# A 4 KB store of zeros ahead of the first rows of a softmax-minus-one-hot kernel

## The chip, the cores and the metric

The kernel runs on one core of one Trainium2 chip. The metric is the device time of one execution in microseconds (us): the median of 3 runs is 1248.03 us (1248.02 to 1248.24). The profile comes from one further execution.

The engines are named as in the profile: PE is TensorE, DVE is VectorE, ACT is ScalarE, POOL is GpSimd, SP is SyncE. SyncE computes nothing here; it issues DMAs. A DMA is issued on the queue of an engine (q1 is SyncE's, q10 ScalarE's in the profile), and the work of both queues runs on the same 16 DMA engines.

## The reference

Logits are 8 x 1024 rows of 8192 float32 numbers, labels one integer for each row.

```python
logits_max = np.max(logits, axis=-1, keepdims=True)
exp_logits = np.exp(logits - logits_max)
softmax = exp_logits / np.sum(exp_logits, axis=-1, keepdims=True)
one_hot[batch_idx, seq_idx, labels] = 1.0
return (softmax - one_hot).astype(np.float32)
```

So 268 MB are read and 268 MB written, and every number is touched by a maximum, an exponential with a sum, a scaling, and a subtraction of 1 where the column is the label.

## The kernel before

**Tiles.** The 8192 rows are cut into T = 64 tiles of 128 rows ("row t" in the code and below: one tile of 128 x 8192 float32, 4.194 MB). Two neighbouring tiles form a block b = t // 2, with j = t % 2. SBUF holds X, three slots of two tiles; block b lives in slot b % 3, so six tiles are on the chip at a time, and tile t uses the memory of tile t - 6.

**Instructions.** All instructions are recorded through the helper `run` (lines 63 to 74): it puts the instruction on an engine in program order, lets it wait on the semaphores in its list, and counts a semaphore up when it ends. So the order within each engine is the order of the calls, and between engines only the listed waits hold. In the profile nearly everything has line L68, that of the helper, and is told apart by engine, operation and tile.

**Before the loop** (lines 77 to 101). ScalarE issues the load of the labels (64 KB as 32 rows of 2 KB). GpSimd sets `ident`, a 32 x 32 tile, to zero (memset), makes it the identity (affine_select), and writes column numbers 0 to 8191 as 16-bit integers (iota) into the memory of X that tile 5 is going to use (`made`). VectorE turns the labels to float (`lab_f`), TensorE transposes them with `ident`, VectorE copies the result out of PSUM (`lab`) and copies `made` into PSUM (`iota`); this last copy needs GpSimd's iota. VectorE's own order is: cast, copy of `lab`, copy of `iota`, and then the maximum of row 0.

**Loads.** SyncE issues the loads of tiles 0 to 5 at once, tile 5 after the copy of `iota`, since `made` lies in its memory. Every later load t waits for the store of tile t - 6. All loads are in order on SyncE's queue, which carries nothing else.

**The loop over the tiles.** For each t, VectorE does the reciprocal of row t's sum, the maximum of row t + 1 (tensor_reduce to `m`), and the subtraction for row t (scalar_tensor_tensor: is the column number equal to the label, minus the scaled row, reversed). ScalarE does the exponential of row t with its sum, issues the store of row t - 1, and scales row t by the reciprocal. The last row is scaled, subtracted and stored in pieces: four column quarters, two stores of half a row. At the end ScalarE waits for the last six tiles' stores.

Of the kernel before, what the change touches and what calls it, by code (L numbers as in the profile page):

```python
# [7 lines left out]
P = 128  # L8
G = 2
SLOTS = 3  # L10


LOADS = "r" * 32
LAST = 4


# [1 line left out]
def kernel(  # L18
# [6 lines left out]
    nc = tc.nc  # L25
# [3 lines left out]
    Act = mybir.ActivationFunctionType  # L29
    Alu = mybir.AluOpType  # L30

    x_nv = logits.flatten_outer_dims()
    o_nv = out.flatten_outer_dims()
    N, V = x_nv.shape
    T = N // P
    B = T // G
    lab_bp = labels.rearrange("a b -> (a b)").rearrange("(b q) -> b q", q=G * P)
    x_b = x_nv.rearrange("(b p j) v -> b p j v", p=P, j=G)
    o_b = o_nv.rearrange("(b p j) v -> b p j v", p=P, j=G)
# [5 lines left out]
    X = const.tile([P, SLOTS, G, V], fp32)  # L45
    lab_raw = const.tile([B, G * P], labels.dtype)
    lab_f = const.tile([B, G, P], fp32)
    ident = const.tile([B, B], fp32)
    lab = const.tile([P, G, B], fp32)

    m, s, r = (const.tile([P, T], fp32, name=n) for n in ("m", "s", "r"))

    iota = psum.tile([P, V], i16)
    lab_ps = iota[:].bitcast(fp32)[:, :T].rearrange("p (j b) -> p j b", j=G)

    with tc.tile_critical():  # L56
        sem = tc.alloc_semaphore
        got = [[sem(f"got{i}{q}") for q in range(2)] for i in range(SLOTS)]
        put = [[sem(f"put{i}{q}") for q in range(2)] for i in range(SLOTS)]
        lab_got, dve, act, pe, pool = (sem(n) for n in ("lab_got", "dve", "act", "pe", "pool"))  # L60
        count = {}

        def run(engine, waits, counter, method, **operands):

            waits = list(dict.fromkeys(waits))
            for w in waits[:-1]:
                engine.wait_ge(*w)
            instruction = getattr(engine, method)(**operands)  # L68
            for w in waits[-1:]:
                instruction._wait_ge(*w)  # L70
            step = 16 if method == "dma_start" else 1
            instruction.then_inc(counter, step)
            count[counter.name] = count.get(counter.name, 0) + step
            return counter, count[counter.name]


        w_raw = run(nc.scalar, [], lab_got, "dma_start", out=lab_raw[:], in_=lab_bp)
        w = run(nc.gpsimd, [], pool, "memset", ap=ident[:], constant=0.0)
        w_ident = run(
            nc.gpsimd, [w], pool, "affine_select",  # L80
            out=ident[:], in_=ident[:], compare_op=Alu.not_equal, fill=1.0,
            base=0, pattern=[[-1, B]], channel_multiplier=1,
        )

        made = X[:, SLOTS - 1, G - 1, :].bitcast(i16)[:, :V]
        w_made = run(
            nc.gpsimd, [], pool, "iota", out=made, pattern=[[1, V]], base=0, channel_multiplier=0
        )
        step = mybir.dt.size(labels.dtype) // 4
        lab32 = lab_raw[:].bitcast(i32).rearrange("b (p j s) -> b j p s", j=G, s=step)  # L90
        w_lab = run(nc.vector, [w_raw], dve, "tensor_copy", out=lab_f[:], in_=lab32[:, :, :, 0])
        for j in range(G):
            w = run(
                nc.tensor, [w_ident, w_lab], pe, "transpose",
                out=lab_ps[:, j, :], in_=lab_f[:, j, :], identity=ident[:],
            )
        w_turned = run(nc.vector, [w], dve, "tensor_copy", out=lab[:], in_=lab_ps)
        w_iota = run(
            nc.vector, [w_turned, w_made], dve, "tensor_scalar",
            out=iota[:].bitcast(i32), in0=made.bitcast(i32), scalar1=0, scalar2=None, op0=Alu.bitwise_or,  # L100
        )


        every, rows = slice(0, P), slice(0, G)
        one = [slice(j, j + 1) for j in range(G)]
        halves = [slice(i, P, 2) for i in range(2)]
        PIECES = {
            "r": [(every, js) for js in one],
            "s": [(ps, js) for js in one for ps in halves],
            "t": [(ps, one[0]) for ps in halves] + [(every, js) for js in one[1:]],  # L110
            "w": [(every, rows)],
        }

        def meets(a, b):

            sets = [[set(range(*d.indices(n))) for d, n in zip(p, (P, G))] for p in (a, b)]
            return all(x & y for x, y in zip(*sets))


        loaded, stored, finished = {}, {}, []  # L120
        last_made = [((every, slice(G - 1, G)), w_iota)]

        def load(b):
            loaded[b] = []
            before = stored.get(b - SLOTS, last_made if b == SLOTS - 1 else [])
            for piece in PIECES[LOADS[b]]:
                ps, js = piece
                free = [w for other, w in before if meets(piece, other)]
                queue = nc.scalar if ps == halves[1] else nc.sync
                w = run(  # L130
                    queue, free, got[b % SLOTS][js.start], "dma_start",
                    out=X[ps, b % SLOTS, js, :], in_=x_b[b, ps, js, :],
                )
                loaded[b].append((piece, w))

        def store(t, done, c=slice(0, V)):
            b, j = divmod(t, G)
            piece = (every, one[j])
            w = run(
                nc.scalar, [done], put[b % SLOTS][j], "dma_start",  # L140
                out=o_b[b, :, j, c], in_=X[:, b % SLOTS, j, c],
            )
            stored.setdefault(b, []).append((piece, w))


        def row(t):
            return X[:, t // G % SLOTS, t % G, :]

        def row_max(t):
            b, j = divmod(t, G)  # L150
            arrived = {w[0].name: w for piece, w in loaded[b] if meets(piece, (every, one[j]))}
            return run(
                nc.vector, arrived.values(), dve, "tensor_reduce",
                out=m[:, t : t + 1], in_=row(t), axis=mybir.AxisListType.X, op=Alu.max, negate=True,
            )


        for b in range(SLOTS):
            load(b)
        w_max = row_max(0)  # L160
        for t in range(T):
            x = row(t)
            label = lab[:, t % G, t // G : t // G + 1]
            w = run(
                nc.scalar, [w_max], act, "activation",
                out=x, in_=x, func=Act.Exp, bias=m[:, t : t + 1], scale=1.0, accum_out=s[:, t : t + 1],
            )
            w_sum = run(nc.vector, [w], dve, "reciprocal", out=r[:, t : t + 1], in_=s[:, t : t + 1])
            if t + 1 < T:
                if (t + 1) % G == 0 and (t + 1) // G >= SLOTS:  # L170
                    load((t + 1) // G)
                w_max = row_max(t + 1)
            if t > 0:
                store(t - 1, finished[t - 1])

            n = 1 if t + 1 < T else LAST
            cols = [slice(i * V // n, (i + 1) * V // n) for i in range(n)]
            scaled = [
                run(
                    nc.scalar, [w_sum], act, "activation",  # L180
                    out=x[:, c], in_=x[:, c], func=Act.Copy, bias=0.0, scale=r[:, t : t + 1],
                )
                for c in cols
            ]
            done = [
                run(
                    nc.vector, [w], dve, "scalar_tensor_tensor",
                    out=x[:, c], in0=iota[:, c], scalar=label, in1=x[:, c],
                    op0=Alu.is_equal, op1=Alu.subtract, reverse1=True,
                )  # L190
                for c, w in zip(cols, scaled)
            ]
            finished.append(done[-1])
        half = V // 2
        store(T - 1, done[LAST // 2 - 1], slice(0, half))
        store(T - 1, done[LAST - 1], slice(half, V))
        for b in range(B - SLOTS, B):
            last = {w[0].name: w for _, w in stored[b]}
            for w in last.values():
                nc.scalar.wait_ge(*w)  # L200


# [28 lines left out]
```

## Time and profile before

| what | value |
|---|---|
| median of 3 runs | 1248.03 us |
| the profiled execution | 1248.17 us, of it 1246.4 us span |
| DVE / ACT / POOL busy | 1121.6 / 919.4 / 7.4 us |
| bytes moved by DMA, mean rate | 536.98 MB, 431 GB/s |
| loads on SP's queue | 64, 4096 KB each, median 24.2 us from issue to landing |
| stores on ACT's queue | 63, 4096 KB each, median 55.1 us; two of 2048 KB |
| the labels' load on ACT's queue | 64 KB, 3.9 us |

The span runs from the first to the last instruction of the program; the execution's own time has some 1.8 us around it. "40 slices" are 40 equal parts of the span, 31 us each, in which a digit is the busy share in tenths. In the groups, the numbers behind the bar are the busy time in us and the mean of one instruction in ns, then the idle time of the engine just before such instructions and what ended it. In a row of the windows there stand the stretch in us, its length, the busy time of PE, PEld, DVE, ACT and POOL with the number of instructions, the granted clock, the DMA share and, last, GB/s. A window counts a DMA packet where it starts, so short windows scatter. The trace also keeps every DMA packet by itself, with its start, duration, bytes and queue; a tile moves as 128 packets of 32 KB, eight on each of the 16 DMA engines, and each transfer ends with one packet of 4 bytes for each engine, which counts the semaphore up.

### The profile page before, as it was taken

The page shows a single profiled execution, that of the slowest core. Times are in us where ns is not written, and L with a number is a line of the kernel's source. Part 1 is how long each engine was busy: PE and PEld are TensorE (multiplying, and loading weights), DVE is VectorE, ACT ScalarE, POOL GpSimd, SP SyncE. Part 2 cuts the span into 40 slices and gives each one's busy share as a digit, 9 for nine tenths or more (in the row PEclk, how much of TensorE's full clock was granted, in tenths as well). Part 3 has the DMA queues.
Part 4 walks back from the last instruction along what each step waited for, and adds up shares of the span by engine and source line. Part 5 has one row for each costly group of instructions (what it writes and reads, how often), then busy time and mean ns, then how long its engine had stood idle before and what let it go on. Part 6 is the DMA issues. An engine that isn't in the chain of part 4 may idle for free.

```text
span 1246.4 us, 597 instructions
## 1 busy us (share of the span) xinstructions
PE 0.4 (0%) x2; PEld 0.3 (0%) x2; DVE 1121.6 (90%) x198; ACT 919.4 (74%) x196; POOL 7.4 (1%) x7
## 2 busy tenths in 40 slices
PE   0000000000000000000000000000000000000000
PEld 0000000000000000000000000000000000000000
DVE  5999999999988989889898898998988989889893
ACT  3888888888767777677767777777777777677772
POOL 2000000000000000000000000000000000000000
DMA  9999999999999999999999999999999999999998
GB/s 406 415 430 433 436 433 430 434 435 433 432 433 434 433 432 433 434 432 433 433 434 432 433 433 433 433 433 433 434 433 431 434 434 433 430 433 436 432 430 387
DMA packets 18628, 536.98 MB, mean 431 GB/s; under 512 B 2080, under 2 KB 2080, under 8 KB 2112
## 3 DMA queue, kind: packets, MB, share of 16 engines
q1 hardware_dynamic: 9216, 268.44, 50.0%
q10 hardware_dynamic: 9408, 268.51, 49.9%
q14 instruction: 4, 0.03, 0.0%
HBM read 268.50 MB, written 268.44 MB: 431 GB/s over the span
## 4 chain that ended last, share of the span: by engine, by line
another core or an unknown queue 69%; DVE 21%; DMA 6%; SPq 1%; ACT 1%; DVEq 0%; issue 0%; PE 0%; ACTq 0%
DVE m L68 10%; DVE X L68 10%; DMA out_dram<-X 4%; DMA X<-in_logits_dram 2%; SPq L68 1%; ACT X L68 1%; DVE iota L68 0%; DMA lab_raw<-in_labels_dram 0%; DVE lab_f L68 0%; DVEq L56 0%; DVE r L68 0%; PE iota L68 0%; ACTq L68 0%; DVE lab L68 0%
## 5 line engine op out<-in xcount | busy, mean ns | idle before, releaser
L68 DVE TENSOR_REDUCE m<-X 128x1 f32<-128x8192 f32 x64 | 555.5, 8680 | 91.4 <-DMA X<-in_logits_dram 91.4
L68 ACT ACTIVATE X<-X,m 128x8192 f32<-128x8192 f32 x64 | 455.8, 7122 | 187.9 <-DVE m L68 187.9
L68 DVE SCALAR_TENSOR_TENSOR X<-iota,lab,X 128x8192 f32<-128x8192 int16 (+1 forms) x67 | 559.8, 8359 | 2.4 <-ACT X L68 2.4
L68 ACT ACTIVATE X<-X,r 128x8192 f32<-128x8192 f32 (+1 forms) x67 | 456.3, 6815 | 116.0 <-DVE r L68 116.0
L68 DVE RECIPROCAL r<-s 128x1 f32<-128x1 f32 x64 | 9.7, 152 | 7.3 <-ACT X L68 7.3
L68 ACT ACTIVATION_READ_ACCUMULATOR X<-X,m 128x1 f32 x64 | 11.9, 187 | 0.0
L68 DVE CAST lab_f<-lab_raw 32x256 f32<-32x256 int32 x1 | 3.6, 3610 | 4.8 <-DMA lab_raw<-in_labels_dram 4.8
L68 POOL IOTA X<- 128x8192 int16 x1 | 6.9, 6944 | 0.0
L68 DVE TENSOR_SCALAR iota<-X 128x4096 int32<-128x4096 int32 x1 | 4.4, 4428 | 0.1
L68 ACT ACT_TABLE_LOAD x1 | 1.3, 1283 | 1.4 <-SPq L56 1.4
L68 DVE COPY lab<-iota 128x64 f32<-128x64 f32 x1 | 0.2, 225 | 0.5 <-PE iota L68 0.5
L68 PE MATMUL iota<-ident,lab_f 32*128 32x32 f32 x2 | 0.4, 299 | 8.5 <-DVE lab_f L68 8.5
L68 PEld LDWEIGHTS iota<-ident,lab_f 32*128 32x128 f32 x2 | 0.3, 196 | 8.5 <-DVE lab_f L68 8.5
L68 POOL TENSOR_SCALAR_AFFINE_SELECT ident<-ident 32x32 f32<-32x32 f32 x1 | 0.2, 203 | 0.1
L68 POOL MEMSET ident<- 32x32 f32 x1 | 0.1, 115 | 0.5 <-SPq L56 0.5
L215 POOL MEMSET const-bfloat16-1.0<- 128x1 bf16 x1 | 0.1, 107 | 0.0
L215 POOL MEMSET const-uint8-127<- 128x1 uint8 x1 | 0.1, 107 | 0.0
L215 POOL MEMSET const-float32-0.0<- 128x1 f32 x1 | 0.1, 104 | 0.2 <-issue 0.2
L215 POOL MEMSET const-float32-1.0<- 128x1 f32 x1 | 0.1, 104 | 0.0
## 6 DMA issues: line engine op xcount, KB each, us to landing
X<-in_logits_dram SPq DMA_DIRECT2D x64, 4096.0 KB, 24.2
out_dram<-X ACTq DMA_DIRECT2D x63, 4096.0 KB, 55.1
out_dram<-X ACTq DMA_DIRECT2D x2, 2048.0 KB, 16.8
lab_raw<-in_labels_dram ACTq DMA_DIRECT2D x1, 64.0 KB, 3.9
```

Of the source, the lines that this page charges most:

```text
L68: instruction = getattr(engine, method)(**operands)
L215: nc = _bacc.Bacc("TRN2", target_bir_lowering=False, num_devices=1)
```

## The change

A third transfer is added to the start. After the labels, ScalarE's queue gets a store of `ident` while it is still all zeros: 32 rows of 128 bytes into the first 32 columns of the first 32 rows of the output. It waits for GpSimd's memset. GpSimd's affine_select, which turns the zeros into the identity, then waits until this store has landed, with a semaphore of its own, `early`. The store of row 0, which writes the same places of the output again with the right numbers, waits for `early` too.

The rest of the diff writes the loop in other functions: loads are issued tile by tile (`load(t)`) in place of block by block, unused ways to cut a load (`PIECES`, `LOADS`) go, and the last row's scalings and subtractions are called in turn.

```diff
+        w_early = run(
+            nc.scalar, [w], early, "dma_start", out=o_nv[0:B, 0:B], in_=ident[:]
+        )
         w_ident = run(
-            nc.gpsimd, [w], pool, "affine_select",
+            nc.gpsimd, [w, w_early], pool, "affine_select",
             out=ident[:], in_=ident[:], compare_op=Alu.not_equal, fill=1.0,
             base=0, pattern=[[-1, B]], channel_multiplier=1,
         )
...
+        def load(t):
+            b, j = divmod(t, G)
+            free = [stored[t - G * SLOTS]] if b >= SLOTS else [w_iota] if t == G * SLOTS - 1 else []
+            loaded[t] = run(
+                nc.sync, free, got[b % SLOTS][j], "dma_start", out=row(t), in_=x_b[b, :, j, :]
+            )
...
         def store(t, done, c=slice(0, V)):
             b, j = divmod(t, G)
...
+            stored[t] = run(
+                nc.scalar, [w_early, done] if t == 0 else [done], put[b % SLOTS][j], "dma_start",
+                out=o_b[b, :, j, c], in_=row(t)[:, c],
+            )
...
+        def by_rows(first, last):
+            for t in range(first, last):
+                row_exp(t)
+                invert(t, t + 1)
+                if t + 1 < T:
+                    if t + 1 >= G * SLOTS:
+                        load(t + 1)
+                    row_max(t + 1)
+                if t > 0:
+                    store(t - 1, finished[t - 1])
+                if t + 1 < T:
+                    row_scale(t)
+                    subtract(t)
...
+        for t in range(G * SLOTS):
+            load(t)
+        row_max(0)
+        by_rows(0, T)
+        quarters = [slice(i * V // 4, (i + 1) * V // 4) for i in range(4)]
+        done = []
+        for c in quarters:
+            row_scale(T - 1, c)
+            done.append(subtract(T - 1, c))
```

Here B is 32, G is 2, SLOTS is 3 and T is 64. `row_exp`, `invert`, `row_max`, `row_scale` and `subtract` each record one instruction, the one that stood in the loop before.

More of the change, by code (lines that the diff above doesn't have):

```diff
@@ L10 @@
 SLOTS = 3
-LOADS = "r" * 32
 LAST = 4
@@ L59 @@
         put = [[sem(f"put{i}{q}") for q in range(2)] for i in range(SLOTS)]
-        lab_got, dve, act, pe, pool = (sem(n) for n in ("lab_got", "dve", "act", "pe", "pool"))
+        lab_got, dve, act, pe, pool, early = (
+            sem(n) for n in ("lab_got", "dve", "act", "pe", "pool", "early")
+        )
         count = {}
@@ L101 @@
         )
[L104 to L117, printed above, removed]
@@ L120 @@
[L120 to L134, printed above, removed]
+        stored, loaded, finished, biggest, summed, inverse, scaled = {}, {}, {}, {}, {}, {}, {}
@@ L136, in store, with row @@
+        def row(t):
+            return X[:, t // G % SLOTS, t % G, :]
+        def load(t):
[4 more added lines that the diff above has]
+            )
         def store(t, done, c=slice(0, V)):
             b, j = divmod(t, G)
[L138 to L141, printed above, removed]
-            )
@@ L143, in store @@
-            stored.setdefault(b, []).append((piece, w))
-        def row(t):
-            return X[:, t // G % SLOTS, t % G, :]
+            stored[t] = run(
+                nc.scalar, [w_early, done] if t == 0 else [done], put[b % SLOTS][j], "dma_start",
+                out=o_b[b, :, j, c], in_=row(t)[:, c],
+            )
         def row_max(t):
[L150 to L153, printed above, removed]
+            biggest[t] = run(
+                nc.vector, [loaded[t]], dve, "tensor_reduce",
@@ L154, in row_max @@
                 out=m[:, t : t + 1], in_=row(t), axis=mybir.AxisListType.X, op=Alu.max, negate=True,
             )
[L158 to L166, printed above, removed]
-            )
[L168 to L193, printed above, removed]
@@ L194, with row_exp @@
-        half = V // 2
[L195 to L200, printed above, removed]
+        def row_exp(t):
+            summed[t] = run(
+                nc.scalar, [biggest[t]], act, "activation", out=row(t), in_=row(t),
+                func=Act.Exp, bias=m[:, t : t + 1], scale=1.0, accum_out=s[:, t : t + 1],
+            )
@@ new lines, in invert, with row_scale, subtract @@
+        def invert(a, z):
+            w = run(nc.vector, [summed[z - 1]], dve, "reciprocal", out=r[:, a:z], in_=s[:, a:z])
+            inverse.update((t, w) for t in range(a, z))
+        def row_scale(t, c=slice(0, V)):
+            scaled[t] = run(
+                nc.scalar, [inverse[t]], act, "activation", out=row(t)[:, c], in_=row(t)[:, c],
+                func=Act.Copy, bias=0.0, scale=r[:, t : t + 1],
+            )
+        def subtract(t, c=slice(0, V)):
+            finished[t] = run(
+                nc.vector, [scaled[t]], dve, "scalar_tensor_tensor",
+                out=row(t)[:, c], in0=iota[:, c], scalar=lab[:, t % G, t // G : t // G + 1],
+                in1=row(t)[:, c], op0=Alu.is_equal, op1=Alu.subtract, reverse1=True,
+            )
+            return finished[t]
@@ new lines @@
+        row_max(0)
[5 more added lines that the diff above has]
+            done.append(subtract(T - 1, c))
+        half = V // 2
+        store(T - 1, done[1], slice(0, half))
+        store(T - 1, done[3], slice(half, V))
+        last = {stored[t][0].name: stored[t] for t in range(T - G * SLOTS, T)}
+        for w in last.values():
+            nc.scalar.wait_ge(*w)
```

## The prediction

> **What bounds the kernel now.** I read the page's 40 slices first, then the costliest groups, the waits (of the DMA queues too), the timeline of the first 90 us and the throughput by window.
>
> The 40 slices and three groups of the page:
>
> ```profile
> DVE  5999999999988989889898898998988989889893
> ...
> DMA  9999999999999999999999999999999999999998
> GB/s 406 415 430 433 436 433 430 434 435 433 432 433 434 433 432 433 434 432 433 433 434 432 433 433 433 433 433 433 434 433 431 434 434 433 430 433 436 432 430 387
> ...
> L68 DVE TENSOR_REDUCE m<-X 128x1 f32<-128x8192 f32 x64 | 555.5, 8680 | 91.4 <-DMA X<-in_logits_dram 91.4
> L68 ACT ACTIVATE X<-X,m 128x8192 f32<-128x8192 f32 x64 | 455.8, 7122 | 187.9 <-DVE m L68 187.9
> L68 DVE SCALAR_TENSOR_TENSOR X<-iota,lab,X 128x8192 f32<-128x8192 int16 (+1 forms) x67 | 559.8, 8359 | 2.4 <-ACT X L68 2.4
> ```
>
> The DMA engines are full from the first slice to the last, at 433 GB/s. A tile of 128x8192 f32 is 4.194 MB, so it takes 4.194/433 = 9.68 us, and a row of work (one load, one store) 19.36 us. VectorE needs 8.68 + 8.74 = 17.4 us a row, which is less. The longest wait of SyncE's queue says the same:
>
> ```profile
> SPq L68 <- DMA out_dram<-X: 1141.3, 58, 57.4
> ```
>
> Each of the last 58 loads waits for the store that frees its slot. The kernel therefore ends when 537 MB have gone through. A delay on an engine counts only where it leaves *both* queues (loads on SyncE's, stores on ScalarE's) without data, or makes the DMA engines move less.
>
> The start, where the change sits, from the timeline (start, duration):
>
> ```profile
> 0.91 0.42 ACTq L68 DMA_DIRECT2D lab_raw<-in_labels_dram  x1
> 0.95 0.12 POOL L68 MEMSET ident<- 32x32 f32 x1 [0.51 <-SPq L56]
> ...
> 1.15 0.20 POOL L68 TENSOR_SCALAR_AFFINE_SELECT ident<-ident 32x32 f32<-32x32 f32 x1
> 1.31 6.94 POOL L68 IOTA X<- 128x8192 int16 x1
> ...
> 4.79 3.61 DVE L68 CAST lab_f<-lab_raw 32x256 f32<-32x256 int32 x1 [4.79 <-DMA lab_raw<-in_labels_dram]
> ...
> 9.25 4.43 DVE L68 TENSOR_SCALAR iota<-X 128x4096 int32<-128x4096 int32 x1
> 13.58 8.68 DVE L68 TENSOR_REDUCE m<-X 128x1 f32<-128x8192 f32 x1
> ...
> 64.29 0.34 ACTq L68 DMA_DIRECT2D out_dram<-X  x1
> ```
>
> The last line is the issue of row 1's store; row 0's goes out at 46.98. And the throughput by window (last column GB/s):
>
> ```profile
> 4.00:44.00 40.00, 0.42 (x2) 0.29 (x2) 31.31 (x7) 20.02 (x4) 4.25 (x1) 1.00 1.00 433
> 44.00:56.00 12.00, 0.00 (x0) 0.00 (x0) 12.00 (x4) 9.03 (x4) 0.00 (x0) 1.00 1.01 393
> ...
> 200.00:1198.00 998.00, 0.00 (x0) 0.00 (x0) 907.73 (x158) 747.25 (x159) 0.00 (x0) 1.00 1.00 433
> ```
>
> There is one dip between the ramp and the tail: 44 to 56 us, where the first store begins. It costs 12 x (1 - 393/433) = 1.1 us. The trace's records of single packets show it on all 16 DMA engines: two load packets of 32 KB in a row take 1.5 to 2.1 us instead of 1.21, and the first packet of the store starts at 52.1, 5.15 us after its issue. When the load queue runs dry later (load 6, issued at 71.48, has its first packet at 75.1), the store packets go on at 1.21 us and nothing is lost. So a queue that starts again costs nothing by itself; only the first store did.
>
> **The change part by part.** Per engine, the loop's instructions, operands and order stay the same on SyncE, ScalarE and VectorE: the loads were already issued row by row on a queue that does nothing else, so moving their place in the program moves no wait. The new code is therefore worth 0, apart from these four edits.
>
> 1. *One DMA on ScalarE's queue.* It waits for the memset (done at 1.07), long before the labels' issue ends (1.33). Its own issue takes 0.34 to 0.42 us; behind it stands the table load (1.28 us) of an engine that is idle until 22.3. Cost 0.
>
> 2. *4 KB in 32 pieces of 128 bytes*, two on each DMA engine. The labels' 2 KB pieces took 0.08 us each when undisturbed, so between 0 (4 KB at 433 GB/s is 0.01 us) and 0.2 us of DMA time. I take 0.1.
>
> 3. *affine_select waits until it has landed, and iota stands behind it on GpSimd.* Call the landing L. Lower bound: as fast as the labels (3.85 us from issue to landing): L = 1.33 + 3.85 = 5.2. Upper bound: as late to begin as row 0's store, 5.15 us, then two load packets of 1.21 between its pieces and its semaphore, and 0.7 to land: L = 9.6, or 10.8 if it meets the 1.2 us stall besides. Between them, by the packets: the labels' semaphore ran at 4.1, one load packet after their data, since the two queues take turns by packet. Piece, piece and semaphore behind that, each one load packet of 1.21 later, are at 5.3, 6.5 and 7.7, and 0.5 to land gives L = 8.2, my value. The iota is then ready at L + 0.1 + 0.20 + 6.94 = 15.4. Today the copy of it starts at 9.25, so the first reduce and all rows behind move by d = L - 1.9 = **6.3 us** (3.3 to 8.9). The transposes need ident at about 8.5 and are hidden behind the iota.
>
> What does d cost? Load 5 waits for that copy, but its turn at the DMA engines comes only at 52: cover 38 us. VectorE is late until its lead over the loads is used up (back to back until about 250 us, then 91.4 us of waiting): hidden. The one narrow place is the end of row 0's store. Seven transfers (loads 0 to 5, store 0) end at 72.3 by the packets. The next data are row 1's store, issued at 64.29 + d, with at least 1.06 us to its first packet (as the labels), and load 6, which waits for store 0 to land. So both queues are dry from d = 72.3 - 64.29 - 1.06 = **6.9 us** on. At d = 6.3: 0 us. At 8.9: 2.0 us, then load 6 fills in.
>
> 4. *Row 0's store has one more wait,* met long before: 0.
>
> The Trainium skill ("DMA: Bandwidth & Descriptors", Anatomy of one DMA) puts the fixed cost of a small DMA at about 2.0 us, most of it the receipt of the write, heaviest for HBM. By that figure alone L would be about 3.3 and d an estimated 1.4; the labels' 3.85 us from issue to landing beside full load packets already speak against it, and by either the time stays.
>
> **Sum.** 0 + 0.1 + 0 + 0, and the 1.1 us of the first store is paid once, early or late: +0.1. If the pieces of 128 bytes are a little slower than that, +0.3. The profiled execution took 1248.17 (span 1246.4 and 1.8 around it), 0.14 above the median of 1248.03; I put the sum on the median: **1248.2 us**.
>
> **The rivals.**
>
> *The first store's 1.1 us goes away* because the small store takes it while the DMA engines are ramping up anyway (first load packets of 1.4 to 1.7 us instead of 1.21). For: it came once, at the first write to the output. Against: engines that stall at 3 us stall loads too. Seven transfers then end at 71.2; row 1's store is ready at 64.29 + 6.3 + 1.06 = 71.7: 0.5 us of the gain is lost again. Time 1247.0 to 1247.6; I say 1247.3.
>
> *Paid twice*: the stall belongs to the first write and, again, to the first full packet of a store. Cost 1.1 to 1.2: 1249.3.
>
> *Slower: the rows start so late that both queues run dry.* Mechanism as in 3, place: the end of row 0's store at 72 us. It decides from d = 6.9, and passes 2.5 us from about d = 11.5, L = 13.4: row 1's store is ready 2.5 us or more after the data end, load 6 only at about 74.3 (2.0 us dry), and in the next round store 2 (issued at 81.6 + 12) comes 1.0 us after 93.7, which makes 3.0 us at d = 12: 1251. Each further us adds to it, up to some 5 us at d = 15. For: no row shows a write of 128 bytes, and row 0's store began 5.15 us late. The Trainium skill (same page, Specifications) says that pieces under 512 bytes are written by reading, modifying and writing; no run here shows it yet, and it would push L up. Against: it needs 12 us for 4 KB.
>
> *It does more than hide the stall*: ramp (0.8 us by the packets), stall (1.1) and the spread between the engines at the end (last landings 1243.3 to 1245.1, 1.3 us lost) all gone would be 3.2 us: 1244.8. Nothing speaks for the last.
>
> **How the numbers follow.** Forecast 0.46 (1248.2, between 1247.8 and 1248.8), stall gone 0.21, paid twice 0.17, dry queues 0.12, more than the stall 0.04. A difference under 0.2%, 2.5 us, is about what a measurement of this kernel can tell from none: the first three lie inside, 0.84. Slower 0.12, faster 0.04. The range takes in the first three and the bounds of d: from 1246.8 (the whole 1.1 us gone) to 1250.6 (0.1, 2.0 us dry and a part of the stall twice).
>
> **What the profile after would show.** (3) The small store's landing near 8.2, affine_select behind it, iota at 8.5 to 15.5, first reduce at about 19.9, row 0's store issued at 53.3. (2) 433 GB/s wherever both queues hold data. A dip to about 393 in the 12 us around row 0's store if the stall stays, at 3 to 8 us if it moved. Rivals: no dip anywhere; dips in both places; a dip at 71 to 75 us. I would be wrong if the loads' pace between 200 and 1198 us left 433, which no part of the change touches, or if the small store landed past 13.

## The result

The changed kernel takes 1251.51 us (median of 8 runs, 1250.97 to 1252.38) against 1248.16 for the kernel before (8 runs, 1247.97 to 1248.25): 3.35 us more, a ratio of 1.0028 with a 95% interval of 1.0019 to 1.0036. The forecast was 1248.2 with a range up to 1250.6; the time lies above it. The profiled execution of the changed kernel took 1250.97 us with a span of 1249.2, so 2.80 us more than that of before: it is the fastest of the eight, and what follows accounts for the 2.8 us of that execution, not for all of the 3.35.

From the page of the changed kernel: the throughput in 40 slices, two groups with the idle time before them, and the issue of the small store.

```profile
GB/s 405 420 390 430 435 435 433 431 431 434 434 435 430 431 434 435 435 429 431 434 436 433 430 431 434 436 433 432 433 430 436 434 433 431 432 435 433 433 432 385
...
L69 DVE TENSOR_SCALAR iota<-X 128x4096 int32<-128x4096 int32 x1 | 4.4, 4427 | 6.1 <-POOL X L69 6.1
...
L69 POOL TENSOR_SCALAR_AFFINE_SELECT ident<-ident 32x32 f32<-32x32 f32 x1 | 0.2, 202 | 8.6 <-DMA out_dram<-ident 8.6
...
out_dram<-ident ACTq DMA_DIRECT2D x1, 4.0 KB, 8.2
```

From the fourth slice on it is the old picture, about 433 GB/s up to the last slice (385, before 387). The third slice (62 to 94 us) has 390 in place of 430. The other lines tell how the change gets there: the small store needs 8.2 us from issue to landing, GpSimd's affine_select stands idle for 8.6 us until then, and VectorE waits 6.1 us for the iota behind it.

The timeline of the same execution (start, duration):

```profile
9.66 0.20 POOL L69 TENSOR_SCALAR_AFFINE_SELECT ident<-ident 32x32 f32<-32x32 f32 x1 [8.60 <-DMA out_dram<-ident]
9.82 6.94 POOL L69 IOTA X<- 128x8192 int16 x1
...
16.80 4.43 DVE L69 TENSOR_SCALAR iota<-X 128x4096 int32<-128x4096 int32 x1 [6.14 <-POOL X L69]
21.14 8.68 DVE L69 TENSOR_REDUCE m<-X 128x1 f32<-128x8192 f32 x1
...
54.53 0.36 ACTq L69 DMA_DIRECT2D out_dram<-X  x1
...
71.84 0.35 ACTq L69 DMA_DIRECT2D out_dram<-X  x1
...
72.38 0.33 SPq L69 DMA_DIRECT2D X<-in_logits_dram  x1
```

The first reduce starts at 21.14 in place of 13.58, the stores of rows 0 and 1 go out at 54.53 and 71.84 in place of 46.98 and 64.29: all rows are 7.55 us late. The last line is the issue of load 6, which waits for row 0's store to land.

Throughput by window, first of the kernel before, then of the changed one (last column GB/s):

```profile
68.00:80.00 12.00, 0.00 (x0) 0.00 (x0) 12.00 (x2) 10.85 (x3) 0.00 (x0) 1.00 1.01 434
```

```profile
56.00:68.00 12.00, 0.00 (x0) 0.00 (x0) 12.00 (x2) 10.87 (x2) 0.00 (x0) 1.00 0.99 401
68.00:80.00 12.00, 0.00 (x0) 0.00 (x0) 12.00 (x3) 9.52 (x3) 0.00 (x0) 1.00 0.95 363
80.00:90.00 10.00, 0.00 (x0) 0.00 (x0) 10.00 (x4) 7.67 (x3) 0.00 (x0) 1.00 0.98 423
90.00:130.00 40.00, 0.00 (x0) 0.00 (x0) 40.00 (x7) 34.05 (x7) 0.00 (x0) 1.00 1.00 428
```

The dip of the first store has gone along with it to 56 to 68 us; a new and larger one stands at 68 to 80.

Since windows count a packet where it starts, I also spread each packet's bytes over its duration; "lost" below is the length of a stretch less the bytes moved in it divided by 433.3 GB/s. By that the changed kernel loses 0.95 us at 44 to 64 us (before: 1.18), **2.36 at 70 to 80** (0.01) and 0.56 at 80 to 130 (0.00). That is 2.7 us more than before, out of 2.8. The 2.36 have two parts. Row 0's store ends its data at 71.6 to 72.0 on the 16 engines, and row 1's store, issued at 71.84, has its first packets at 72.7 to 72.9: nothing moves for about a microsecond (1.02 us lost from 70 to 74). Then load 6, issued at 72.38, joins: the store packets that begin near 75.2 take 1.7 to 2.3 us in place of 1.21, and on most engines the next load packet up to 2.6 (1.34 us lost from 74 to 80).

One point of the description ahead of the prediction is to be made exact: the small store's 32 rows belong to tiles 0 and 1 by turns, so the stores of row 0 and of row 1 write them again.

### The profile page after: what moved, and what is told of

The parts are those of the page before. It is cut to its first block, busy times and chain, and to the rows that moved or that the text cites. A ratio compares the mean times of both kernels' runs of the same rounds, so it can differ in the third digit from the quotient of the medians.

```text
span 1249.2 us, 599 instructions
## 1 busy us (share of the span) xinstructions
PE 0.4 (0%) x2; PEld 0.3 (0%) x2; DVE 1118.2 (90%) x198; ACT 919.3 (74%) x196; POOL 7.4 (1%) x7
## 4 chain that ended last, share of the span: by engine, by line
another core or an unknown queue 64%; DVE 25%; DMA 7%; SPq 1%; ACT 1%; POOL 1%; DVEq 0%; issue 0%; ACTq 0%
DVE m L69 12%; DVE X L69 12%; DMA out_dram<-X 4%; DMA X<-in_logits_dram 2%; SPq L69 1%; ACT X L69 1%; DMA out_dram<-ident 1%; POOL X L69 1%; DVE iota L69 0%; DVEq L55 0%; DVE r L69 0%; ACTq L69 0%; POOL ident L69 0%; ACTq L211 0%
## 5 line engine op out<-in xcount | busy, mean ns | idle before, releaser
L69 DVE CAST lab_f<-lab_raw 32x256 f32<-32x256 int32 x1 | 0.4, 373 | 4.8 <-DMA lab_raw<-in_labels_dram 4.8
```

## The experiments

Theory A: the small store costs nothing by itself; making affine_select and the iota wait for it makes all rows late, and late rows let the two queues run out near 72 us. Theory B: the small store itself costs, by its 128-byte pieces or by what it leaves in the DMA engines. Every time below is compared with runs of the kernel before on the same chip, whose medians were 1248.12 to 1248.20.

**The store without the wait** (own_zeros in the table below).

```diff
+        w_zeros = run(nc.vector, [], dve, "memset", ap=zeros[:], constant=0.0)
         w_early = run(
-            nc.scalar, [w], early, "dma_start", out=o_nv[0:B, 0:B], in_=ident[:]
+            nc.scalar, [w_zeros], early, "dma_start", out=o_nv[0:B, 0:B], in_=zeros[:]
         )
...
-            nc.gpsimd, [w, w_early], pool, "affine_select",
+            nc.gpsimd, [w], pool, "affine_select",
```

> The small store stays second on ScalarE's queue, but reads a tile of zeros of its own, so nothing on GpSimd waits for it; only row 0's store does. Theory A (the cost is the late start of the rows, through affine_select and iota): first reduce back at 13.6 us, row 0's store issued at 47.0, time that of before, 1248.2 (1247.8 to 1248.6). Theory B (the cost is the small store itself: its 128-byte pieces, or what they leave behind in the DMA engines): 1251.5, that of the changed kernel. Theory C (the first write to the output stalls the DMA engines once, whoever makes it): no dip at 48 to 52 us, and a dip at 6 to 10 us.

Measured: 1248.21 us, ratio 1.0001 (0.9992 to 1.0010). Its timeline and windows:

```profile
1.38 0.44 ACTq L70 DMA_DIRECT2D out_dram<-zeros  x1
...
13.58 8.68 DVE L70 TENSOR_REDUCE m<-X 128x1 f32<-128x8192 f32 x1
```

```profile
44.00:56.00 12.00, 0.00 (x0) 0.00 (x0) 12.00 (x4) 9.02 (x4) 0.00 (x0) 1.00 1.02 404
56.00:68.00 12.00, 0.00 (x0) 0.00 (x0) 12.00 (x3) 10.15 (x3) 0.00 (x0) 1.00 1.00 431
68.00:80.00 12.00, 0.00 (x0) 0.00 (x0) 12.00 (x2) 10.87 (x3) 0.00 (x0) 1.00 1.00 431
```

A store of the same size and shape in the same place of the queue, and no loss that stands clear of the spread of the runs: theory B falls as the cause of the 3.35 us. The dip at the first large store stays (404 at 44 to 56 us, 1.07 us lost), so an earlier small write to the output does not take it away: theory C, that it belongs to the first write whoever makes it, falls too.

**The wait kept, the iota ahead of it** on GpSimd (iota_first: the iota's call moved above affine_select's).

> The changed kernel with GpSimd's iota ahead of affine_select, which still waits for the small store: only the transposes wait. Theory A: ident is ready at 9.9, the copy of lab at 10.4, so the rows move by about 1.4 us instead of 7.6, and the time is that of before, 1248.2 (1247.8 to 1248.8). Theory B: 1251.5.

Measured: 1248.87 us (1248.45 to 1250.52), ratio 1.0007 (0.9998 to 1.0016); first reduce at 15.05, 1.5 us late. By the medians, most of the loss is gone with most of the delay. The time lies just above the range that theory A had given (1247.8 to 1248.8), and the spread is wide; the next kernels follow that up. The profiled execution took 1250.52 us and is the slowest of the eleven, so its packets in the table below are not those of a median run.

**Late rows without the small store.** The kernel before, with VectorE making extra copies ahead of the real one of the iota; the tuple of columns sets the delay. The six expectations stand in the order late_75 (whose edit is shown), late_44, late_15, late_30, late_62 and late_120; a name gives the delay aimed at in tenths of a us.

```diff
+        for n in (4096, 2800):
+            w_turned = run(
+                nc.vector, [w_turned, w_made], dve, "tensor_scalar",
+                out=iota[:].bitcast(i32)[:, :n], in0=made.bitcast(i32)[:, :n],
+                scalar1=0, scalar2=None, op0=Alu.bitwise_or,
+            )
```

> The kernel before, without the small store, with VectorE copying the iota in two extra pieces (4096 and 2800 columns) ahead of the real copy, so that the first reduce starts about 7.5 us later. Theory A: the same loss as the change, 1250.7 to 1252.4, with both queues dry near 72 us and the load packets stretched when load 6 starts. Theory B: 1248.2.

> The same with one extra copy (4096 columns), so 4.5 us later. Theory A with a limit near 6 to 7 us, below which the queues overlap: 1248.2 (1247.8 to 1248.8). A loss in proportion to the delay (3.35 us for 7.55): 1250.2. Theory B: 1248.2.

> The kernel before with one extra copy of 1350 columns on VectorE: rows 1.5 us later, no small store. The last kernel with iota first had its rows 1.5 us later and 0.7 us more time, with a wide spread (1248.45 to 1250.5). If that belongs to the delay (load 6 is issued just as loads and row 0's store run out together): 1248.5 to 1249.5, with a wide spread, load packets and store packets stretched at 75 to 80 us on some DMA engines and not on others. If it belongs to the small store: 1248.2, narrow.

> The kernel before with one extra copy of 2750 columns: rows about 3.1 us later, between the kernel that lost 1.3 us (1.5 us later) and the one that lost nothing (4.5 us later). A loss that hangs on whether a transfer is issued just as its queue runs out: anywhere from 1248.2 to 1249.6, with the loss in the packets between 68 and 100 us equal to the whole difference. A smooth curve through the others would give about 1248.9.

> Rows about 6.4 us later. Theory A with the limit at 6.9 us for dry queues: row 1's store is issued at about 70.7, just ahead of row 0's end, so little or nothing is dry: 1248.2 to 1249.2. In proportion to the delay: 1251.0.

> Rows about 12 us later. Theory A: both queues are dry at 72 us until load 6 comes (issue 72.4 and 1.0 to its first packet, 1.5 to 2 us), a queue that starts again costs about 1.1 more each time, and a round later it comes once more, smaller: 1252 to 1254.5, clearly above the 1251.2 at 7.5 us. If the loss were one fixed step past the limit: 1251.2.

**The small store with other numbers of rows**, the wait kept: 16 rows of `ident` (rows16, whose edit is shown), or 64 rows of a tile of its own (rows64).

```diff
-            nc.scalar, [w], early, "dma_start", out=o_nv[0:B, 0:B], in_=ident[:]
+            nc.scalar, [w], early, "dma_start", out=o_nv[0 : B // 2, 0:B], in_=ident[: B // 2, :]
```

> The changed kernel with a small store of 16 rows in place of 32, so one piece of 128 bytes on each DMA engine in place of two. If each piece waits for one load packet: landed at 8.4, first reduce at 19.9 (delay 6.3), and the time of the kernel whose rows were 6.6 us late, 1249.9 (1249.3 to 1250.4). If the landing is a fixed time of a small write: landed at 9.6, 1251.5.

> The changed kernel with a small store of 64 rows, from a tile of zeros of its own, and affine_select still waiting for it: four pieces on each DMA engine. If each piece waits for one load packet: landed at 12.0, first reduce at 23.5 (delay 10), time between the 1251.2 at 7.7 and the 1253.5 at 12.2: 1252.4 (1251.8 to 1253). If fixed: 1251.5.

Measured, in order of the delay. "Late" is the first reduce against 13.58; "lost" is by the packets of the profiled execution, in us, around the first store, at 70 to 80 and at 80 to 130 us; "more" is the median against the runs of before that belong to it, 1248.12 to 1248.20.

| kernel | late | lost 44-64 | 70-80 | 80-130 | median | more |
|---|---|---|---|---|---|---|
| before | 0 | 1.18 | 0.01 | 0.00 | 1248.16 | 0 |
| own_zeros | 0.0 | 1.07 | 0.01 | 0.00 | 1248.21 | 0.1 |
| iota_first | 1.5 | 1.01 | 0.52 | 0.56 | 1248.87 | 0.7 |
| late_15 | 1.7 | 0.75 | 0.13 | 0.95 | 1249.39 | 1.3 |
| late_30 | 3.1 | 0.57 | 0.01 | 0.69 | 1249.17 | 1.1 |
| late_44 | 4.5 | 0.73 | 0.00 | 0.01 | 1248.25 | 0.1 |
| rows16 | 6.3 | 1.17 | 1.02 | 0.84 | 1250.97 | 2.8 |
| late_62 | 6.6 | 0.66 | 1.37 | 0.52 | 1249.89 | 1.8 |
| the change | 7.6 | 0.95 | 2.36 | 0.56 | 1251.51 | 3.4 |
| late_75 | 7.7 | 0.78 | 2.41 | 0.31 | 1251.20 | 3.1 |
| rows64 | 11.5 | 0.10 | 3.18 | 2.51 | 1252.93 | 4.7 |
| late_120 | 12.2 | 0.15 | 2.91 | 3.30 | 1253.49 | 5.4 |

Four expectations were missed. late_62 came out at 1249.89 where theory A had 1248.2 to 1249.2, rows16 at 1250.97 where it had 1249.3 to 1250.4, and iota_first as said; in rows64 the time fits (1252.93), but the small store landed at 13.58, not at 12.0. In late_15 the time fits too, but most of the loss came at 80 to 130 us, not at 75 to 80. For iota_first, late_15 and late_30 the 95% intervals of the ratio reach 1.000 (0.9998 to 1.0016, 1.0000 to 1.0017, 0.9999 to 1.0017); in each of the three, all runs but one at most lie above every run of before, by tenths of a microsecond.

The delay alone, without the small store, gives the change's loss in the same window (late_75, ratio 1.0025, 1.0014 to 1.0035):

```profile
21.29 8.68 DVE L68 TENSOR_REDUCE m<-X 128x1 f32<-128x8192 f32 x1
```

```profile
68.00:80.00 12.00, 0.00 (x0) 0.00 (x0) 12.00 (x3) 9.68 (x3) 0.00 (x0) 1.00 0.92 352
```

and 4.5 us of delay give none there (late_44, ratio 1.0001, 0.9992 to 1.0010):

```profile
68.00:80.00 12.00, 0.00 (x0) 0.00 (x0) 12.00 (x4) 9.65 (x2) 0.00 (x0) 1.00 0.99 429
```

So theory A holds for the place of the loss and for most of its size. But the loss is neither a proportion of the delay nor a step at 6.9 us. At 1.5 to 3.1 us something is lost, at 4.5 nothing, from 6.3 on the loss grows. rows16 tells most, since its rows are as late as the prediction had put those of the change:

```profile
8.39 0.20 POOL L69 TENSOR_SCALAR_AFFINE_SELECT ident<-ident 32x32 f32<-32x32 f32 x1 [7.32 <-DMA out_dram<-ident]
...
19.86 8.68 DVE L69 TENSOR_REDUCE m<-X 128x1 f32<-128x8192 f32 x1
...
70.57 0.35 ACTq L69 DMA_DIRECT2D out_dram<-X  x1
...
72.60 0.33 SPq L69 DMA_DIRECT2D X<-in_logits_dram  x1
```

```profile
68.00:80.00 12.00, 0.00 (x0) 0.00 (x0) 12.00 (x4) 9.03 (x4) 0.00 (x0) 1.00 1.02 407
```

Row 1's store is issued at 70.57, and from 70 to 74 us only 0.09 us is lost: the two queues do not run dry together, just as the limit of 6.9 us said. From 74 to 80, where load 6 joins, 0.93 is lost, and 0.77 from 90 to 100. So a transfer that starts after its own queue has run out of data (the load queue's last data ended at 66.1) can cost about a microsecond without any time in which nothing moves.

The delay does not settle the time to a microsecond. late_62 has nearly the same delay as rows16, 6.6 us, and takes 1.1 us less. At 70 to 130 us the two lose the same in their profiled executions (1.90 and 1.86 us); 0.5 us of the difference lies at the first store, and why, no run shows.

The landing of the small store, 8.32 us with one piece on each engine and 9.60 with two, moves by 1.28, one load packet (1.21 us). In rows64 it is 13.58; there the labels landed 2.7 us later as well (7.48 in place of 4.78), and from the first piece (7.7) to the landing it took 5.9 us in place of the change's 3.3 (6.3 to 9.6), so 2.6 us for two more pieces.

**The handover at 72 us loosened, the delay kept** (split_first). Handover means here the time around 72 us in which row 0's store ends and row 1's store and load 6 begin. The changed kernel with row 0's store and load 6 in two column halves; the first half of load 6 waits for the first half of the store alone.

```diff
+            if t == G * SLOTS:
+                first_half[t] = run(
+                    nc.sync, [first_half[0]], got_a, "dma_start",
+                    out=row(t)[:, halves[0]], in_=x_b[b, :, j, halves[0]],
+                )
...
+            if t == 0:
+                first_half[0] = run(
+                    nc.scalar, [w_early, done], put_a, "dma_start",
+                    out=o_b[b, :, j, halves[0]], in_=row(t)[:, halves[0]],
+                )
+                c = halves[1]
```

> The changed kernel (rows 7.6 us late) with row 0's store and load 6 cut into two column halves, so that the first half of load 6 can start when half of the store has landed, at about 67 us in place of 72.4. If the loss comes from both queues running out together near 72 us, no delay is taken away here but the load queue holds data again before the store ends: 0.5 to 1.2 us of loss in the 12 us from 68 in place of 2.35, and 1249.0 to 1250.3. If the late rows cost in another way: 1251.5.

Measured: 1250.17 us (1249.97 to 1250.39), ratio 1.0016 (1.0007 to 1.0025), though the rows were 8.9 us late in its profiled execution (the labels landed 2.5 us later there, and the small store with them, at 10.97).

```profile
68.00:80.00 12.00, 0.00 (x0) 0.00 (x0) 12.00 (x3) 10.17 (x3) 0.00 (x0) 1.00 1.01 433
80.00:90.00 10.00, 0.00 (x0) 0.00 (x0) 10.00 (x2) 7.93 (x3) 0.00 (x0) 1.00 1.00 433
90.00:130.00 40.00, 0.00 (x0) 0.00 (x0) 40.00 (x9) 33.14 (x7) 0.00 (x0) 1.00 1.00 412
```

The dip at 68 to 80 is gone, 433, though the rows are even later: the loss there is the handover's. Most of it comes back one round later (2.2 us lost at 80 to 130, against 0.56 in the changed kernel), where row 2's store (issued at 90.53) comes just as row 1's has ended (90.57), so the time falls by 1.3 us only.

**What the 1.1 us of the first store belong to.** Three kernels, from the kernel before or from own_zeros, with their edits in part: all stores on SyncE's queue (one_queue); an early store of 256 KB in place of 4 (warm_256k); load 5 on ScalarE's queue behind the exponential of row 0 (load5_act).

```diff
...
-                nc.scalar, [done], put[b % SLOTS][j], "dma_start",
+                nc.sync, [done], put[b % SLOTS][j], "dma_start",
...
```

```diff
-    zeros = const.tile([B, B], fp32)
+    zeros = const.tile([P, 512], fp32)
...
-            nc.scalar, [w_zeros], early, "dma_start", out=o_nv[0:B, 0:B], in_=zeros[:]
+            nc.scalar, [w_zeros], early, "dma_start", out=o_b[0, :, 0, 0:512], in_=zeros[:]
```

```diff
...
+            if t == 0:
+                piece, free = held.pop()
+                ps, js = piece
+                wl = run(
+                    nc.scalar, free, got[SLOTS - 1][G - 1], "dma_start",
+                    out=X[ps, SLOTS - 1, js, :], in_=x_b[SLOTS - 1, ps, js, :],
+                )
```

> The kernel before with all stores moved to SyncE's queue, behind the loads that are already there (order from row 0 on: store t, then load t + 5), so no second queue ever starts beside a running one. If the 1.1 us at the first store belongs to a second queue that starts: no dip at 48 to 62 us, 1247.1. If it belongs to the first full write: the dip stays, 1248.2. Against both: a load that waits for its store holds up the next store, and if the single queue runs out then, 1250 or more.

> As own_zeros, but the early store is 128 rows of 2 KB (256 KB), which row 0's store writes again. If the 1.1 us at the first large store belong to the first time that all 16 engines write to the output in bulk: they move to about 6 to 12 us, 48 to 52 us is undisturbed, time 1248.15 + 0.6 for the bytes = 1248.8. If they belong to a store that starts beside a running load stream after its queue was empty: the dip stays at 48 us, and one more of up to 1.1 us comes early, 1248.8 to 1249.9.

> The kernel before with load 5 issued on ScalarE's queue behind the exponential of row 0 (at about 29.4 us), so that this queue already moves data when row 0's store is issued at 47. If a queue that starts beside a running one costs the 1.1 us whatever it moves: the dip moves to 30 us, 1248.2. If only stores cost it: a dip remains at 48 to 52 us, 1248.2. If it is neither (a store behind a running load on its own queue is free and a load that starts beside loads is free): no dip, 1247.1.

Measured: 1252.14, 1248.89 and 1248.24 us (ratios 1.0030, 1.0006, 1.0001). The packets show the loss at the first large store in all three: 1.18 us at 44 to 64 (one queue), 1.09 (256 KB early), 0.77 (load 5 on ScalarE's queue). In the last, load 5's start at 25.8 beside running loads lost 0.03 us between 20 and 28, and the early 256 KB lost 0.08 between 8 and 20. So it is neither the first write to the output nor a second queue that starts. Nor does it need an empty queue: in one_queue load 5 stood right ahead of row 0's store in the same queue, with data until 62.4. (load5_act does not test this: load 5 was issued at 22.30 there, not at about 29.4, and had ended at 44.3, before the store's issue at 46.97.)

It does not come with every first store, though. In rows64 and late_120 row 0's store has its first packets at 61.1, when each DMA engine is just done with its loads, and only 0.10 and 0.15 us are lost; in the other kernels of the table the loss is 0.57 to 1.18. Where loads were still to run for microseconds it came each time, but its size is not explained, and which part of the DMA engine it belongs to, no run shows. No version beat the kernel before. The one with one queue takes 4 us more: by the packets it loses 1.6 us more than the kernel before from 64 to 450 us, and 2.2 more behind 1198, at the end.

## Why the prediction was wrong

- **What bounds the kernel** held: 433 GB/s from 200 to 1198 us in both, VectorE's delay hidden behind the DMA, no loss from the rewritten loop (own_zeros has it too). The forecast's own signs of being wrong, a pace other than 433 and a landing past 13 us, did not show; the sign of the rival "dry queues", a dip at 71 to 75 us, did. That rival, with a chance of 0.12, had the place and a part of the mechanism. That its 1251 comes near the 1251.51 is luck: it asked for a delay of about 12 us, and at 7.55 its sum gives 0.65 us of dry time, 1248.9. At 12.2 us (late_120) the measured loss is 5.4 us, where it had 3.0.
- **The small store's own cost** (part 2, 0 to 0.2 us): right. Its pieces take 0.01 us each, and own_zeros is 0.06 us above before, inside the spread of its runs.
- **The delay** (part 3): L was put at 8.2 and came out at 9.6, the upper bound of the case without a stall; d was 7.55, not 6.3. (By the prediction's own terms, 15.4 less 9.25, its d would be 6.2; the 0.1 changes nothing.) The first piece went at 6.3, one load packet later than I had it. The piece and semaphore behind it cost one packet each as put, which the kernel with 16 rows confirms. With 7.55 the prediction's own limit of 6.9 is passed, and one microsecond of dry time follows (1.02 lost).
- **The step that failed** is the sentence "a queue that starts again costs nothing by itself; only the first store did". It rested on one event, load 6 of the kernel before, and that event was not what it was taken for: load 6 was issued at 71.48, while load 5 still had data on every engine (its last packets end between 71.5 and 72.3).

```profile
71.48 0.33 SPq L68 DMA_DIRECT2D X<-in_logits_dram  x1
```

  In the changed kernel load 6 is issued at 72.38, 7.6 us after the load queue's last data (64.7), and 1.34 us is lost where it joins; 0.56 more is lost where row 2's store takes over. The kernel with 16 rows has exactly the forecast delay of 6.3 and 0.09 us of loss from 70 to 74, and still takes 2.8 us more; late_62, at 6.6, takes 1.8 more. So even with L right the forecast of 1248.2 would have been wrong: the sum had put the price of a restart, the first packets of a transfer after its queue has had no data for a while, at nothing, and that was missing from it, not only 1.3 us of delay.
- **The first store's 1.1 us**: paid once, as forecast; it moved with row 0's store to 56 us (0.95 lost). The rivals "goes away" and "paid twice" (at the start) did not come about.

What is not settled: when a restart costs and when it does not. In late_44 load 6 was issued 4.0 us after the load queue's last data and lost nothing. In split_first the load queue had been empty for 4.9 us when the first half of load 6 was issued (67.60), and the store queue for 0.5 us when row 1's store was (73.21); from 70 to 80 us that kernel lost 0.05. The six kernels that lost 0.7 us or more at 74 to 80 us (rows16, late_62, the change, late_75, rows64, late_120) have two things in common: the load queue had been empty for 6.5 to 10.2 us when load 6 was issued, and row 1's store was issued less than 2 us before row 0's data ended, or after that, so that both queues handed over together. No run takes these apart. A long empty time alone is not enough, since ScalarE's queue in load5_act had been empty for about 20 us when load 5 was issued on it, and 0.03 us was lost. Nor is a queue that is empty at the issue needed: row 2's store in late_15 was issued 3.6 us before row 1's data ended, and 0.95 us was lost there.

In iota_first the engines differ: those whose row 0 store ended before about 71.8 us show no stretched packets when load 6 joins, most of the later ones do. That fits a dependence on tenths of a microsecond and the wider spread of runs (1.4 us in the changed kernel, 0.3 before), but no run isolates it. Two kinds of start, with the labels landing at about 4.7 or about 7.3 us, may add to the spread (rows16 has the early kind, late_62 the late one); the runs without a profile can't tell.

## What to carry to other kernels

A dummy transfer is not dear by its bytes but by what is made to wait for it: here 4 KB cost 0.1 us with a buffer of their own and 3.35 us when GpSimd's iota stood behind their landing. Beside a full queue the small DMA landed one large packet later for each piece on an engine (1.28 us for one more piece). In a kernel bound by DMA, a delay at the start is not hidden just because the transfers have slack later: look for the moment at which the first store, the first slot that comes free and the second store hand over. Here a restart cost between nothing and 1.3 us, and in the changed kernel 2.4 us were lost where both queues handed over together; put a range like that into the sum, not nothing.

## What the runs showed of the hardware

- Restarts, as above: about 1.0 us without any packet between the issue of a store into idle engines and its data (0.86 us from issue to first packet), and up to 1.3 us more in stretched packets where the other queue joins (0 in late_44, 1.34 in the changed kernel).
- The Trainium skill ("DMA: Bandwidth & Descriptors", Queues, rings and completion order) says that a DMA engine takes turns between its queues packet by packet; the 1.28 us for one more piece of 128 bytes agrees. The fixed cost of about 2.0 us for a small DMA that the Trainium skill gives ("DMA: Bandwidth & Descriptors", Anatomy of one DMA) is a fit for DMAs issued from GpSimd; the store here, issued from ScalarE beside full load packets, took 8.2 us.
- The cast of the labels took 3.61 us in the kernel before, beside GpSimd's iota, and 0.37 us in the changed one, where the iota starts later:

```profile
4.80 0.37 DVE L69 CAST lab_f<-lab_raw 32x256 f32<-32x256 int32 x1 [4.80 <-DMA lab_raw<-in_labels_dram]
```

  In late_75 it began at 7.39 and took 1.01. Both long ones end at 8.40, just behind the iota's end at 8.25. The Trainium skill ("SBUF — State Buffer", SBUF: two separate sides) describes ports that VectorE and GpSimd share, which one instruction holds until it ends; for VectorE it says so of instructions in a mode that uses two ports, or with two inputs in SBUF. The three rows agree with it; in which mode the cast ran, none of them shows.
